# The weights of the query and key norms: a load with strides of zero, or a matmul that spreads one row

## The chip, the cores and the metric

The kernel runs on one core of a Trainium2 chip. The metric is the device time of one launch in microseconds, lower is better. The profile is one execution, taken by the hardware profiler; its engines are PE (TensorE's matmuls), PEld (TensorE's weight loads), DVE (VectorE), ACT (ScalarE), POOL (GpSimd) and SP (SyncE, which here only issues loads). SPq and ACTq are the issues of loads and stores by SP and ACT. L942 is line 942 of the kernel before.

## The reference

A backbone of two layers over 256 latent tokens and 256 context tokens of width 1024. Each layer has three token mixers on one normalised input (attention, an RWKV recurrence, a short convolution), a gated merge, and a mixture of 16 experts. All is float32. The part that the change touches is the norm of the queries and keys in the attention: each head of 64 values is divided by its root mean square and multiplied by 64 weights, which all 8 query heads share, and all 2 key heads share another 64.

```python
def _rms_norm(x, gain):
    xf = x.astype(jnp.float32)
    y = xf * lax.rsqrt(jnp.mean(xf * xf, axis=-1, keepdims=True) + NORM_EPS)
    return (y * gain.astype(jnp.float32)).astype(x.dtype)
...
        q = _rms_norm(q.reshape(b, t, ATT_HEADS, ATT_HEAD_DIM), q_gain)
        k = _rms_norm(k.reshape(b, t, ATT_KV_HEADS, ATT_HEAD_DIM), k_gain)
```

q_gain and k_gain have the shape (2, 64): one row of 64 float32 values, 256 bytes, for each layer.

## The kernel before, in words

One loop runs over the two layers. A layer computes the input projection, piece by piece: SP loads a piece of 128 columns of w_in (L337, tile w), ACT and DVE or POOL split it into a high and a low half (L102 and L103, whi and wlo), and TensorE multiplies (L106 to L108 in layer 0, L321 in layer 1). Between these pieces the RWKV recurrence runs, and the matmuls of the adaLN vectors (L188), whose weights come in two loads at a time (L185, tile adaw, three buffers). Query, key and value rows go to DRAM as they are made (L771, tensor qkd).

Behind the recurrence the attention begins, at L916. ACT issues the load of the rotary tables (L924, tile rope). Six times SP loads rows of qkd back (L932, tile qs, or ql in layer 1 where half of the rows is not needed), TensorE turns them with four (or two) transposes (L935) into a PSUM tile of the ring "sm", which has three buffers, and ACT or DVE copies that out (L938, tile qkv). Then the weights of the norms are loaded by ACT into gn, a tile of 128 partitions by 10 heads by 64 (L939 to L942). The source has a stride of zero over partitions and over heads, so that each partition gets the query weights eight times and the key weights twice:

```python
for h0, h1, nm in ((0, 8, "q_gain"), (8, 10, "k_gain")):
    gsrc = a[nm][l]
    nc.scalar.dma_start(gn[:, h0:h1], bass.AP(tensor=gsrc.tensor, offset=gsrc.offset, ap=[[0, 128], [0, h1 - h0], [1, 64]]))
```

ACT squares the rows (L952), DVE sums them (L953) and takes the reciprocal root (L955), and the rows are scaled by it (L964) and by gn (L969 on latent tokens, L979 on context tokens). The rotary embedding follows (L975 to L977), the split of queries (L981, L982) and keys (L989, L991), transposes (L986, L995; L987 and L996 copy them out), and the scores, the softmax and the products with the values (L1005 to L1026). Beside it the gates of the merge are projected with the same pieces of w_in (L761 and L762 finish and store one), SP fetches the other mixers' outputs (L912, tile ob_), the merge's weights (L1065, L1067, tile cw or cwt), and in layer 1 the first weights of the experts (L866, tile we). ACT also issues the load of the router's weights (L1055, tile wr).

The order on each engine is made when the program is built: a scheduler places the instructions of all these parts beside each other, by its own estimates. A load of ACT thus need not stand where its line stands: those of L924, L942 and, in layer 0, L1055 are placed long before the transposes of L935. On the chip each engine runs its list in order, and an instruction that waits holds up all behind it on its engine.

Of the kernel before, what the change touches and what calls it, by code (L numbers as in the profile page):

```python
# [9 lines left out]
F32 = mybir.dt.float32  # L10
# [3 lines left out]
AF = mybir.ActivationFunctionType  # L14
# [40 lines left out]
def build(tc, a, out):  # L55
    nc = tc.nc
    V, S, G, P = nc.vector, nc.scalar, nc.gpsimd, nc.tensor
    es = ExitStack()

    def pool(name, bufs=1, **kw):  # L60
        return tc.tile_pool(name=name, bufs=bufs, reuse_waits="tile", **kw)
# [5 lines left out]
    def ps(shape, tag):  # L67
        n = {"mm": 1, "mf": 2, "sm": 3, "ch": 2}[tag]
        return psp.tile(shape, F32, name="ps_" + tag, tag=tag, bufs=n)
# [5 lines left out]
    one = ck[:, C_ONE:C_ONE + 1]  # L75
# [214 lines left out]
    for l in range(2):  # L290
# [53 lines left out]
        with pool(f"n1{l}") as pl:  # L344
# [8 lines left out]
            else:  # L353
# [11 lines left out]
                for j in range(8):  # L365
                    pt = ps([128, T], ("sm", "ch", "sm", "mf")[j % 4])
                    h = pl.tile([128, T], F32, name="nh", bufs=4)
                    for s, c0 in STREAM:
                        for t in range(2):
                            P.matmul(pt[:, c0 + t * 128:c0 + t * 128 + 128], acc[:, c0 // 128 + t, j * 128:(j + 1) * 128], dg[:, c0 // 128 + t],  # L370
                                     start=True, stop=True)
# [7 lines left out]
        with er:  # L379
            pr = er.enter_context(pool(f"r{l}"))  # L380
# [535 lines left out]
        with ExitStack() as er:  # L916
            pr = er.enter_context(pool(f"a{l}"))
# [19 lines left out]
                    c = t * 128 - (512 if lat and i == 0 else 0)  # L937
                    (S.copy if (t + i) % 2 else V.tensor_copy)(raw[i][:, :, c:c + 128], pt[:, 2 * i:2 * i + 2])  # L938
            gn = pr.tile([128, 10, 64], F32, name="gn")  # L939
            for h0, h1, nm in ((0, 8, "q_gain"), (8, 10, "k_gain")):  # L940
                gsrc = a[nm][l]
                nc.scalar.dma_start(gn[:, h0:h1], bass.AP(tensor=gsrc.tensor, offset=gsrc.offset, ap=[[0, 128], [0, h1 - h0], [1, 64]]))  # L942
            qT = xp.tile([128, 8, NW], F32R, name="qT", tag="x")
            nrm = pr.tile([128, 3, 10, 64], F32, name="nrm", tag="PT")
            kT = pr.tile([128, 2, 2, T], F32R, name="kT")
# [3 lines left out]
            for tt in range(4):  # L949
                h0 = 8 if lat and tt < 2 else 0  # L950
# [5 lines left out]
            for tt in range(4):  # L956
                is_lat = tt >= 2
                hasq = is_lat or not lat
                h0 = 0 if hasq else 8
# [37 lines left out]
            for tt in range(2 if lat else 0, 4):  # L997
                nk = 4 if tt >= 2 else 2
                pov = ps([128, 512], "mm")
                for kv in range(2):  # L1000
                    PT = pr.tile([128, 4, 4, 128], F32, name="PT", bufs=PTB[l])
                    for p in range(4):
                        sc = ps([128, 512], "ch")
                        for q in range(2):
                            P.matmul(sc[:, :nk * 128], qT[:, 4 * kv + p, tt * 128 - n0:(tt + 1) * 128 - n0], kT[:, kv, q, :nk * 128],  # L1005
                                     start=(q == 0), stop=(q == 1))
# [11 lines left out]
                    for kt in range(nk):  # L1018
                        for ph in range(2):
                            P.matmul(pov[64 * ph:64 * ph + 64, 256 * kv:256 * kv + 256].rearrange("p (a q) -> p a q", a=2), rawv(kt, 640 + 64 * kv, 704 + 64 * kv),  # L1020
                                     PT[:, kt, ph::2],
                                     start=(kt == 0), stop=(kt == nk - 1), skip_group_check=True)
# [27 lines left out]
        with ExitStack() as er:  # L1050
# [54 lines left out]
            pr = esr.enter_context(pool(f"rt{l}", side="right"))  # L1105
# [12 lines left out]
            for si in range(NS):  # L1118
                for j in range(8):
# [3 lines left out]
                             start=True, stop=True, skip_group_check=True)  # L1123
# [177 lines left out]
        with ExitStack() as er:  # L1301
# [5 lines left out]
            for e in range(16):  # L1307
                ecur[0] = e
                pgu = []
                for _ in range(2):  # L1310
                    pp = ps([128, FW], "mf")
                    for j2 in range(4):
# [5 lines left out]
                        for jj in range(2):  # L1318
                            j = j2 * 2 + jj
                            for g in range(NG):  # L1320
                                P.matmul(pp[M * g:M * g + M], xe[e // 4][:, j, e % 4], w[:, jj, g * FW:(g + 1) * FW],  # L1321
                                         start=(j == 0), stop=(j == 7), skip_group_check=True)
# [10 lines left out]
                for j2 in range(4):  # L1333
                    w = wload()
                    for jj in range(2):
                        j = j2 * 2 + jj
                        fg, q = j // nq, j % nq
                        for g in range(NG):
                            P.matmul(pd[M * g:M * g + M], hT2[:, q, M * fg:M * fg + M], w[:, jj, g * FW:(g + 1) * FW],  # L1339
                                     start=(j == 0), stop=(j == 7), skip_group_check=True)  # L1340
# [88 lines left out]
```

## Time and profile before

| | us |
|---|---|
| three runs, median | 2376.88 |
| three runs, lowest and highest | 2373.63, 2391.97 |
| profiled execution, its own time | 2388.95 |
| profiled execution, span of its instructions | 2387.2 |

The two stretches that matter are the beginnings of the attention, at about 535 us in layer 0 and at about 1737 us in layer 1. A window gives, for a stretch, the busy time of each engine, the mean clock that TensorE was granted (1.00 is 2.4 GHz, 0.50 is 1.2 GHz), the mean busy share of the core's 16 DMA engines, and what they moved. In a timeline, the brackets at the end of a row hold the idle time before it and what ended it. The chain is the work that ended last, followed back from the program's end: it names at each time what the program waited for.

### The profile page before, as it was taken

How to read it: one execution, taken by the hardware profiler on the slowest of the kernel's cores; microseconds unless marked ns; L12 is line 12 of the kernel's file. 1: busy time of each engine (PE TensorE's matmuls, PEld its weight loads, DVE VectorE, ACT ScalarE, POOL GpSimd, SP SyncE). 2: the span in 40 equal slices, each digit the busy share in tenths (PEclk: the TensorE clock that was granted, in tenths of full speed). 3: DMA queues.
4: the chain of work that ended last, by engine and by line, in shares of the span. 5: the costliest groups of instructions: out<-in, count | busy, mean ns of one | idle time of the engine just before them, and what ended most of it. 6: DMA issues, size and time to landing. Idle time of an engine off the chain costs nothing.

```text
span 2387.2 us, 44154 instructions
## 1 busy us (share of the span) xinstructions
PE 2063.1 (86%) x18187; PEld 1307.5 (55%) x18187; DVE 988.9 (41%) x2525; ACT 702.3 (29%) x1481; POOL 211.3 (9%) x225
## 2 busy tenths in 40 slices
PE   6999999997999989999987999899958987676665
PEld 3766666664678943433322887777746943232222
DVE  4757475634746421211102768567456621000001
ACT  3442424223532522211102653433434421010001
POOL 1000000003223400000000100000132500000000
PEclk7999999998999999999999999789979988777866
DMA  8443333247258699999999344234365889999997
GB/s 278 121 124 94 100 100 95 84 124 223 67 181 265 200 362 363 419 420 419 420 420 367 107 120 143 63 111 144 104 183 162 280 347 417 416 416 417 417 417 304
DMA packets 343365, 585.73 MB, mean 245 GB/s; under 512 B 23550, under 2 KB 206588, under 8 KB 342908
## 3 DMA queue, kind: packets, MB, share of 16 engines
q1 hardware_dynamic: 326928, 567.69, 65.1%
q10 hardware_dynamic: 16236, 15.22, 1.9%
q8 instruction: 143, 2.34, 0.4%
q14 instruction: 58, 0.48, 0.1%
HBM read 563.44 MB, written 19.40 MB: 244 GB/s over the span
## 4 chain that ended last, share of the span: by engine, by line
PE 45%; DMA 24%; DVE 6%; ACT 2%; issue 2%; POOL 1%; SPq 1%; DVEq 0%; ACTq 0%; POOLq 0%
PE ps_mf L1321 9%; DMA we<-in_exp_down_dram 8%; DMA we<-in_exp_up_dram 6%; PE ps_mf L321 5%; DMA we<-in_exp_gate_dram 5%; PE ps_mm L1339 4%; PE ps_mf L106 3%; PE ps_mf L107 3%; PE ps_mf L108 3%; PE ps_mm L321 2%; DMA adaw<-in_ada_w_dram 2%; PE ps_ch L1163 2%; PE ps_mf L188 1%; PE ps_mm L1020 1%; PE ps_sm L534 1%
## 5 line engine op out<-in xcount | busy, mean ns | idle before, releaser
L1321 PE MATMUL ps_mf<-we,xe 128*32 128x256 f32 (+1 forms) x3040 | 414.1, 525 | 98.8 <-DMA we<-in_exp_up_dram 52.8
L1321 PEld LDWEIGHTS ps_mf<-we,xe 128*32 128x32 f32 (+1 forms) x3040 | 135.8, 133 | 341.3 <-issue 150.3
L1339 PE MATMUL ps_mm<-we,hT 128*32 128x256 f32 (+1 forms) x1536 | 201.9, 518 | 47.9 <-DMA we<-in_exp_down_dram 34.4
L102 ACT ACTIVATE whi<-w 128x512 fp32r<-128x512 f32 x236 | 147.7, 629 | 246.8 <-PE ps_mf L107 70.8
L1326 DVE TENSOR_TENSOR hid<-hid,ps_mf 128x512 f32<-128x512 f32 (+1 forms) x32 | 17.7, 554 | 443.2 <-PE ps_mf L1321 442.5
L103 DVE TENSOR_TENSOR wlo<-w,whi 128x512 fp32r<-128x512 f32 x195 | 134.0, 690 | 110.6 <-ACT whi L102 99.6
L321 PE MATMUL ps_mf<-hT,whi 128*128 128x256 f32 x736 | 157.2, 307 | 7.5 <-ACT whi L102 5.3
L1339 PEld LDWEIGHTS ps_mm<-we,hT 128*32 128x32 f32 (+1 forms) x1536 | 68.1, 133 | 164.5 <-issue 71.6
L106 PE MATMUL ps_mf<-hhi,whi 128*128 128x512 f32 x344 | 151.5, 440 | 1.3 <-ACT qs L770 0.5
L107 PE MATMUL ps_mf<-hlo,whi 128*128 128x512 f32 x344 | 142.3, 414 | 0.0
L108 PE MATMUL ps_mf<-hhi,wlo 128*128 128x512 f32 x344 | 141.3, 411 | 1.0 <-issue 1.0
L1345 DVE TENSOR_TENSOR yg<-ps_mm,g2p 128x512 f32<-128x512 f32 (+1 forms) x32 | 17.9, 558 | 275.7 <-PE ps_mm L1339 275.7
L321 PEld LDWEIGHTS ps_mf<-hT,whi 128*128 128x128 f32 x736 | 121.8, 203 | 17.3 <-ACT whi L102 5.7
L321 PE MATMUL ps_mf<-hT,wlo 128*128 128x256 f32 x368 | 109.7, 309 | 2.8 <-POOL wlo L103 1.8
L188 PE MATMUL ps_mf<-adaw,cs 128*32 128x256 f32 x640 | 82.2, 412 | 20.2 <-DMA adaw<-in_ada_w_dram 15.9
L1349 ACT COPY ye<-yg 32x512 f32<-32x512 f32 (+1 forms) x64 | 32.6, 509 | 222.9 <-DVE yg L1345 221.0
L1331 ACT ACTIVATE hT<-ps_sm 128x512 f32<-128x512 f32 (+1 forms) x32 | 15.7, 490 | 243.4 <-PE ps_sm L1330 243.4
L106 PEld LDWEIGHTS ps_mf<-hhi,whi 128*128 128x128 f32 x344 | 66.2, 193 | 24.7 <-issue 4.5
L321 PEld LDWEIGHTS ps_mf<-hT,wlo 128*128 128x128 f32 x368 | 72.5, 202 | 10.6 <-POOL wlo L103 2.6
L108 PEld LDWEIGHTS ps_mf<-hhi,wlo 128*128 128x128 f32 x344 | 66.6, 193 | 17.5 <-issue 3.8
L107 PEld LDWEIGHTS ps_mf<-hlo,whi 128*128 128x128 f32 x344 | 66.7, 194 | 14.4 <-issue 4.3
L321 PE MATMUL ps_mm<-hT,whi 128*128 128x256 f32 x368 | 70.5, 299 | 0.9 <-POOL hm L387 0.4
(472 smaller groups left out, 3789.9 us busy)
## 6 DMA issues: line engine op xcount, KB each, us to landing
we<-in_exp_down_dram SPq DMA_DIRECT2D x123, 1024.0 KB
we<-in_exp_gate_dram SPq DMA_DIRECT2D x118, 1024.0 KB
we<-in_exp_up_dram SPq DMA_DIRECT2D x117, 1024.0 KB
w<-in_w_in_dram SPq DMA_DIRECT2D x228, 256.0 KB
adaw<-in_ada_w_dram SPq DMA_DIRECT2D x160, 256.0 KB
we<-in_exp_gate_dram SPq DMA_DIRECT2D x40, 256.0 KB
adaw<-in_ada_w_dram SPq DMA_DIRECT2D x16, 512.0 KB
cw<-in_w_out_dram SPq DMA_DIRECT2D x32, 256.0 KB
```

What stands on the lines that cost most here:

```text
L102: S.activation(hi, src, AF.Copy)
L103: (eng or G).tensor_tensor(lo, src, hi.bitcast(F32), op=ALU.subtract)
L106: P.matmul(o, lh[0], rh[0], start=first, stop=False)
L107: P.matmul(o, lh[0], rh[1], start=False, stop=False)
L108: P.matmul(o, lh[1], rh[0], start=False, stop=last)
L188: P.matmul(pm[32 * g:32 * g + 32], cs[:, j, :], ws[g // 2][:, g % 2], start=True, stop=True, skip_group_check=True)
L321: P.matmul(o[:, 256 * s - c0:256 * s - c0 + 256], w_[:, j], hT[s][x][:, k], start=first and i == 0 and 256 * s == c0, stop=last and i == 2 ...
L534: P.matmul(pa[h][:, u, :nr], bkh(u4 * 4 + u, h), ARu[hh, u4 * 4 + u, :nr], start=True, stop=True)
L1163: P.matmul(pg, htok[si][:, t, j * 128:(j + 1) * 128], oh[:, t].rearrange("p e c -> p (e c)"), start=(t == 0), stop=(t == 1))
L1321: P.matmul(pp[M * g:M * g + M], xe[e // 4][:, j, e % 4], w[:, jj, g * FW:(g + 1) * FW], start=(j == 0), stop=(j == 7), skip_group_check=True)
L1339: P.matmul(pd[M * g:M * g + M], hT2[:, q, M * fg:M * fg + M], w[:, jj, g * FW:(g + 1) * FW], start=(j == 0), stop=(j == 7), skip_group_che ...
L1349: (S.copy, V.tensor_copy)[(g + si) % 2](ye[32 * eg:32 * eg + 32, si, g * FW:(g + 1) * FW], yg[p0:p0 + 32])
```

## The change

The row of 64 query weights and the row of 64 key weights are each loaded once, into one partition (tile gr). A matmul with a stationary operand of one row of ones (a column of the constants, read 128 times) and gr as the moving operand puts a copy of both rows into each partition of a PSUM tile (pgn, ring "sm"). Two ACT copies write them to gn, one reading the query row eight times, the other the key row twice. Behind it nothing is changed; from L943 on the lines of the changed file are four further down, so that L952 of before is its L956.

```diff
             gn = pr.tile([128, 10, 64], F32, name="gn")
-            for h0, h1, nm in ((0, 8, "q_gain"), (8, 10, "k_gain")):
-                gsrc = a[nm][l]
-                nc.scalar.dma_start(gn[:, h0:h1], bass.AP(tensor=gsrc.tensor, offset=gsrc.offset, ap=[[0, 128], [0, h1 - h0], [1, 64]]))
+            gr = pr.tile([1, 2, 64], F32, name="gr")
+            pgn = ps([128, 2, 64], "sm")
+            for i, (h0, h1, nm) in enumerate(((0, 8, "q_gain"), (8, 10, "k_gain"))):
+                nc.scalar.dma_start(gr[:, i], a[nm][l][None, :])
+            P.matmul(pgn.rearrange("p i x -> p (i x)"), one[0:1].to_broadcast([1, 128]), gr.rearrange("p i x -> p (i x)"), start=True, stop=True)
+            S.activation(gn[:, 0:8], pgn[:, 0:1].to_broadcast([128, 8, 64]), AF.Copy)
+            S.activation(gn[:, 8:10], pgn[:, 1:2].to_broadcast([128, 2, 64]), AF.Copy)
             qT = xp.tile([128, 8, NW], F32R, name="qT", tag="x")
```

On ACT in layer 0 this stands at the loads, before the change (thd_226 is the DRAM tensor of the gates):

```order
L924 DMA rope<-in_const_dram 128x256
L762 DMA thd_226<-th 128x512
L942 DMA gn<-in_q_gain_dram 128x8x64
L942 DMA gn<-in_k_gain_dram 128x2x64
L1055 DMA wr<-in_w_router_dram 128x8x16
L102 ACTIVATE whi<-w_6018 128x512
```

and this with the change:

```order
L924 DMA rope<-in_const_dram 128x256
L762 DMA thd_226<-th 128x512
L943 DMA gr<-in_q_gain_dram 1x64
L943 DMA gr<-in_k_gain_dram 1x64
L1059 DMA wr<-in_w_router_dram 128x8x16
L102 ACTIVATE whi<-w_6018 128x512
```

The loads keep their place; each writes one partition and not 128. In layer 1 it is the same between rope and L761, with no wr behind it.

On TensorE in layer 1, with the change, the new matmul stands behind the last group of L935 (qs is the tile of rows of qkd; hT and whi, wlo are the operands of the projection):

```order
L321 MATMUL ps_mf<-hT,whi 128x256 x2
L935 MATMUL ps_sm<-ck,qs 128x128 x4
L321 MATMUL ps_mf<-hT,wlo 128x256
L321 MATMUL ps_mf<-hT,whi 128x256 x2
L935 MATMUL ps_sm<-ck,qs 128x128 x4
L944 MATMUL ps_sm<-gr,ck 128x128
L321 MATMUL ps_mf<-hT,wlo 128x256
```

L944 is the only instruction that TensorE has more. In layer 0 it stands likewise behind the sixth group of L935, ahead of L108.

On ACT in layer 1, with the change, the two copies stand behind the last copy of L938 and ahead of the second square (here L956):

```order
L938 COPY qkv_16657<-ps_sm 128x2x128
L956 ACTIVATE nrm<-qkv_16656 128x128
L938 COPY qkv_16656<-ps_sm 128x2x128
L945 ACTIVATE gn<-ps_sm 128x512
L946 ACTIVATE gn<-ps_sm 128x128
L956 ACTIVATE nrm<-qkv_16656 128x128
L102 ACTIVATE ohC<-ob__17205 128x256
```

In layer 0 they stand ahead of the third of four squares. In both layers some instructions of the attention and of the projection beside it have changed places behind this point.

## Rows read from the trace of the kernel before

**Rows 1.** The page, busy time of each engine and its share of the span
```profile
PE 2063.1 (86%) x18187; PEld 1307.5 (55%) x18187; DVE 988.9 (41%) x2525; ACT 702.3 (29%) x1481; POOL 211.3 (9%) x225
```

**Rows 2.** Windows of layer 0: stretch, length, busy of engines, clock, DMA share, GB/s
```profile
543.30:554.30 11.00, 0.00 (x0) 0.00 (x0) 1.29 (x2) 1.63 (x3) 0.00 (x0) 0.72 0.40 117
554.30:558.30 4.00, 3.99 (x13) 2.76 (x14) 0.85 (x2) 0.65 (x2) 0.77 (x2) 0.50 0.95 305
558.30:660.00 101.70, 92.14 (x503) 63.98 (x501) 75.00 (x185) 55.33 (x134) 32.67 (x28) 0.98 0.45 144
```

**Rows 3.** Windows of layer 1, columns: PE, PEld, DVE, ACT, POOL, clock, DMA, GB/s
```profile
1740.30:1755.40 15.10, 0.00 (x0) 0.00 (x0) 0.28 (x1) 0.00 (x0) 0.00 (x0) 0.58 0.29 85
1755.40:1759.60 4.20, 4.17 (x20) 4.17 (x21) 0.85 (x2) 1.38 (x3) 1.28 (x1) 0.50 0.82 239
1759.60:1843.00 83.40, 64.84 (x407) 51.26 (x407) 60.96 (x125) 41.52 (x98) 27.68 (x26) 0.89 0.65 198
```

**Rows 4.** Timeline of PE at both places: start us, us, instruction, idle before
```profile
542.64 0.62 PE L188 MATMUL ps_mf<-adaw,cs 128*32 128x256 f32 x4
554.31 1.07 PE L188 MATMUL ps_mf<-adaw,cs 128*32 128x256 f32 x4 [11.05 <-DMA adaw<-in_ada_w_dram]
...
1740.00 0.28 PE L321 MATMUL ps_mf<-hT,wlo 128*128 128x256 f32 x1
1755.43 0.69 PE L935 MATMUL ps_sm<-ck,ql 128*128 128x128 f32 x2 [15.16 <-DMA ql<-qkd]
```

**Rows 5.** Timeline of SP's issues, layer 0, then layer 1
```profile
536.13 5.86 SPq L185 DMA_DIRECT2D adaw<-in_ada_w_dram  x2
...
1739.16 15.16 SPq L932 DMA_DIRECT2D ql<-qkd  x4
```

**Rows 6.** DMA queues, 1739.5 to 1749, then 538.5 to 549: packets, MB, share
```profile
q10 hardware_dynamic: 698, 0.18, 7.0%
q1 hardware_dynamic: 63, 0.03, 1.2%
...
q10 hardware_dynamic: 734, 0.19, 6.6%
q1 hardware_dynamic: 29, 0.06, 2.0%
```

**Rows 7.** Timeline of ACT's issues, layer 0, then layer 1
```profile
534.83 0.45 ACTq L942 DMA_DIRECT2D gn<-in_q_gain_dram  x1
537.32 0.39 ACTq L942 DMA_DIRECT2D gn<-in_k_gain_dram  x1
537.74 7.06 ACTq L1055 DMA_DIRECT2D wr<-in_w_router_dram  x1
...
1737.11 0.46 ACTq L942 DMA_DIRECT2D gn<-in_q_gain_dram  x1
1737.99 0.39 ACTq L942 DMA_DIRECT2D gn<-in_k_gain_dram  x1
```

**Rows 8.** Pieces of the chain that ended last: start us, us, what
```profile
509.25 2.87 DMA adaw<-in_ada_w_dram
...
572.24 4.66 DMA ob__7113<-oRd
...
577.56 0.64 ACT nrm L952
...
1758.16 4.83 DMA ob__17274<-oCd
...
1763.34 0.73 ACT nrm L952
```

**Rows 9.** Lines L935, L987 and L989: shortest, median, longest ns of one
```profile
L935 PE MATMUL ps_sm<-ck,qs x32: 270/273/477, 555.3 to 1761.4; 128*128 128x128 f32 x32
...
L987 ACT ACTIVATE qT<-ps_sm x12: 591/596/606, 592.2 to 1796.5; 128x512 fp32r<-128x512 f32 x12
L989 ACT ACTIVATE ks<-nrm x16: 292/294/310, 589.7 to 1793.4; 128x128 fp32r<-128x128 f32 x16
```

## The prediction

> **What bounds the kernel now.** I read the share of each engine first: TensorE is busy for 86% of the span [rows 1], so what a small change is worth depends on where TensorE stands still. I then read windows of a few microseconds around the two loads that the change replaces, one pair in each layer. In layer 0 TensorE does nothing at all between 543.3 and 554.3 us, and in layer 1 nothing between 1740.3 and 1755.4 us [rows 2, 3]. In the second stretch no engine does more than one small operation, and the DMA engines are busy for 0.29 of it only. So nothing is the bound there: everything waits for something that moves no data.
>
> The timeline says for what. In layer 0 the matmul of L188 sits idle for 11.05 us until its adaw load has landed; in layer 1 the transpose of L935 sits idle for 15.16 us until the first ql has landed [rows 4]. Both loads are ordinary ones of SP, and SP had asked for them in time: at 536.13 and 538.00 (two issues merged in one row, 5.86 us long) and from 1739.16 on [rows 5]. The four ql issues of layer 1 took 15.16 us together, so SP itself was held up while it issued. What ran meanwhile is in the DMA views of the two stretches [rows 6]: 698 packets on q10 with 0.18 MB, which is 256 bytes a packet, against 63 packets on q1; in layer 0, 734 against 29. A row of 64 float32 is 256 bytes, so these packets are the gain loads of L942, which ACT issued at 534.83 and 537.32, and at 1737.11 and 1737.99 [rows 7]. They were 1,280 packets a layer (128 partitions times 10 heads), they went through at 698 in 9.5 us, about 73 per us, and together they kept 7% of 16 engines busy, about one engine of the sixteen. At that rate 1,280 take 17.5 us, which covers both stalls. While they pass, SP's loads hardly move. I take that as the cause; how the two queues come to hold each other up, these rows do not tell.
>
> **The change part by part.** It removes the 1,280 packets of each layer and puts two loads of 64 numbers in their place, issued by ACT at the same two places of its order. The sum for one layer after the other, against the profiled execution's own time, 2388.95 us:
>
> Layer 0. The waiting L188 needs the second adaw of the pair that was asked for at 538.00. How long such a load takes when nothing is in its way is bounded by two pieces of the chain: 2.87 us at 509.25, and 4.83 us for a load in a full queue at 1758.16 [rows 8]. It then lands between 540.9 and 542.8, before TensorE gets to it at 543.26, so all of the 11.05 us goes. What is late next is TensorE itself. It also came out of the stall at half its clock: 0.50 was granted for 554.3 to 558.3, with 3.99 us of TensorE work in it [rows 2]; in 558.3 to 660 the grant was 0.98. That level came after the idle stretch, and without it the same work takes 2.0 us less. Layer 0: 11.05 + 2.0 = 13.05 us. Its other end is 11.05, if the clock falls anyway.
>
> Layer 1. The first ql is asked for at 1739.16 and lands at 1742.03 with the shorter latency, 1743.99 with the longer. TensorE is out of work at 1740.28, so 1.75 (or 3.71) us of waiting stays and 15.16 - 1.75 = 13.4 us goes (or 11.45). I take 13.4, because two loads of weights at most stand ahead of ql on SP's queue. The half clock (0.50 from 1755.4 to 1759.6, with 4.17 us of work) is worth less here: the chain soon leaves TensorE for a load that SP issues at 1758.16 [rows 8], so only the 2.7 us from 1755.43 on count, and I put 1.0 us on it, between 0 and 2.1. Layer 1: 14.4 us.
>
> Added, per layer: one 128 x 128 matmul (L944 of the changed file) behind the last group of L935; the same shape at L935 is 0.27 us with 0.14 us of weight load beside it [rows 9], so 0.3 us on TensorE, nought if it falls into a gap. Two ACT copies out of PSUM: a 128 x 512 one takes 0.60 us at L987 and a 128 x 128 one 0.29 us at L989 [rows 9], so 0.9 us. They read one row of 64 repeated eight times (and twice), which no row of before shows on ACT; I bound them by 0.9 us and twice that. They stand on ACT ahead of the squares of L952, and the chain runs through L952 in both layers, at 577.56 and at 1763.34 [rows 8]; so I count them in full. Both layers: 2 x (0.3 + 0.9) = 2.4 us, between 0 and 4.2.
>
> What else waits: L944 is in TensorE's order and waits for gr; behind it stand the L108 or L321 matmuls and, over them, everything. The two gr loads take the place of issues at 534.83 and 537.32, and the first group of L935 comes at 555.3, or 544.3 with the stall out of between, with five more groups and much of the projection behind it until L944 [rows 7, 9]; a load takes 2.87 to 4.83 us, so the wait is nought. In layer 1 the lead runs from 1737.99 to 1742.03 and over all groups of L935, which take from 1755.43 to 1761.4 [rows 4, 9], so about 10 us, still enough. pgn takes a third of the "sm" buffers until the two copies are done; the next users of that ring are the transposes of L986, which stand behind the whole norm. The load wr of layer 0 (L1055), which was held for 7.06 us while ACT issued it, goes out at once. The scheduler places work of the attention stages a little differently (some 40 places on ACT and 60 on TensorE); I cost that at nothing on the mean and allow 3 us either way.
>
> Sum: 13.05 + 14.4 - 2.4 = 25.05 us. All that follows hangs on these two points, since no engine and no load made headway in the stalls that could be late instead. So 2388.95 - 25 = 2363.9 us for the profiled execution. That one lies 12.1 us above the median of the three runs, 2376.88, which range from 2373.63 to 2391.97; the stall has no reason to differ between them, so I take the 25 us from the median: 2351.8, that is 2352 us, or 1.05% less. About 1%, some 24 us, is what a measurement of this kernel can tell from no change, and the forecast is hardly beyond that.
>
> **Rivals.** The stall is not the gain loads' doing. The packets kept one engine's worth of sixteen busy, and nothing shows that this alone must hold SP's loads; then the time stays at 2376.88 plus the 2.4 us of added work at most, 2377 to 2379. Against it: the same loads stand at the same place in both layers, and in layer 1 no wr load stands behind them. The Trainium skill, in "DMA: Bandwidth & Descriptors", section "Issuing engines are not separate DMA queues", says that loads issued from SP and ACT run on the same sixteen engines and interleave. By that rule q1's packets would take turns with the gain packets, and the stall would be another's. The trace does not agree: 63 packets of q1 beside 698 [rows 6].
>
> Part is given back. The stage behind each stall is the attention, which runs on waits between DVE, ACT and TensorE and on loads. If the longer latency holds in layer 1 (11.45), the clock falls anyway (no 3.0) and the added work is 4.2, the gain is 11.05 + 11.45 - 4.2 = 18.3 us and the time 2358.6; if one of the two stalls stays in another shape, it is about 13 - 1.2, so 2365.
>
> More comes back: layer 0 has pieces of 4.66 us at 572.24 and, in layer 1, of 4.83 us at 1758.16 [rows 8], loads behind the backlog that the stall left. If they fall to 2.87 us, the gain is 25 + 1.8 + 2.0 = 29 us, 2348; with no added cost on the chain, 2345.6.
>
> Slower: the other order of the attention stage. TensorE is idle there for 101.70 - 92.14 = 9.6 us in layer 0 and 83.40 - 64.84 = 18.6 us in layer 1 [rows 2, 3], 28 us. A copy or a transpose that is queued one step later lengthens each of these waits. If the idle time doubles, that costs 28 us against 25 and the time is 2380; it decides from 25 us more on. Against it: the moved instructions are few, and none but L944 to L946 is new.
>
> **How the numbers follow.** The forecast (both stalls go, 20 to 28 us) has 0.62, more than that 0.10, part given back 0.20, no effect 0.05, slower 0.03. The line of 1% lies at 23.8 us, inside the forecast: I put 0.47 of its 0.62 beyond it and, with the 0.10, 0.57 on faster by over 1%; the slower rival at 2380 is itself within 1%, of its 0.03 half reaches beyond, which I round to 0.02; the rest, 0.41, is within 1%. The range goes down to 2340 (the largest gain, 2345.6, less the 3 us by which a run lay under the median, and 2 of reordering) and up to 2370 (one stall left, 2365, and 5 us of scatter), so it leaves out no effect, slower and the tails, some 0.15.
>
> **What would show it.** In the changed profile: no idle stretch of TensorE over 4 us at the adaw and ql loads; SP issues there of 0.3 to 0.4 us each; no 256-byte packets in hundreds on q10; wr issued in under 1 us in layer 0; a granted clock of 1.00 through both places; two new ACT copies of 0.6 and 0.3 us. I am wrong if an idle stretch of over 8 us stands at either place still, or if it is gone and the span is less than 15 us shorter.

## The result, and the profile after

The changed kernel took 2354.11 us (median of four runs, 2348.76 to 2359.97), beside 2383.33 us for the kernel before on the same chip (four runs, 2373.63 to 2391.97): a ratio of 0.9883, with a 95% interval of 0.9851 to 0.9916. The profiled execution took 2359.37 us, its span is 2357.6 us, against 2388.95 and 2387.2 before: 29.6 us less.

TensorE is busy for 7.7 us less than before [rows 1], which is 0.4% of its work; the other 21.9 us are time in which it stood still. Line of the page with the share of the engines, changed kernel:

```profile
PE 2055.4 (87%) x18191; PEld 1299.7 (55%) x18191; DVE 993.1 (42%) x2525; ACT 703.5 (30%) x1485; POOL 208.8 (9%) x225
```

Timeline of PE, changed kernel: the place of the wait in layer 0, the longest wait for adaw behind it, then the first ql of layer 1.

```profile
541.28 0.64 PE L188 MATMUL ps_mf<-adaw,cs 128*32 128x256 f32 x8
...
553.47 0.62 PE L188 MATMUL ps_mf<-adaw,cs 128*32 128x256 f32 x4 [1.71 <-DMA adaw<-in_ada_w_dram]
...
1727.45 0.69 PE L935 MATMUL ps_sm<-ck,ql 128*128 128x128 f32 x2 [1.98 <-DMA ql<-qkd]
```

The waits of 11.05 and 15.16 us of [rows 4] are gone. In layer 0 the matmuls that stood on either side of the wait, at 542.64 and 554.31 us, now run as one row of eight without a break; the 1.71 us stand at a later L188, which waited 1.16 us before. In layer 1, 1.98 us stand where 15.16 were. SP's timeline, same two issues as in [rows 5]:

```profile
534.47 2.48 SPq L185 DMA_DIRECT2D adaw<-in_ada_w_dram  x2
...
1724.12 2.43 SPq L932 DMA_DIRECT2D ql<-qkd  x4
```

The two issues of adaw took 0.33 us each, with a wait for a semaphore between them. Four issues of ql took 2.43 us together instead of 15.16, 0.32 to 0.90 us each. ACT's issues, to be read beside [rows 7]: the two small loads, and wr behind them, which was held for 7.06 us before.

```profile
533.17 0.30 ACTq L943 DMA_DIRECT2D gr<-in_q_gain_dram  x1
533.51 0.28 ACTq L943 DMA_DIRECT2D gr<-in_k_gain_dram  x1
535.93 0.40 ACTq L1059 DMA_DIRECT2D wr<-in_w_router_dram  x1
```

DMA queues of 1723 to 1728 in the changed kernel: packets, MB, share of 16 engines.

```profile
q1 hardware_dynamic: 1587, 1.02, 69.6%
q10 hardware_dynamic: 110, 0.09, 5.4%
```

In 5 us SP's queue (q1) moved 1,587 packets; before it was 63 in 9.5 us [rows 6]. The new instructions, by line, shortest, median and longest ns of one:

```profile
L944 PE MATMUL ps_sm<-gr,ck x4: 270/320/371, 559.6 to 1733.7; 1*128 1x128 f32 x4
...
L945 ACT ACTIVATE gn<-ps_sm x2: 598/599/600, 560.2 to 1734.0; 128x512 f32<-128x512 f32 x2
...
L946 ACT ACTIVATE gn<-ps_sm x2: 272/274/277, 560.7 to 1734.5; 128x128 f32<-128x128 f32 x2
```

L944 shows as two instructions a layer and not as one, 0.48 us together. A copy that reads one PSUM row of 64 eight times takes what a plain copy out of PSUM of that size takes, 0.60 us [rows 9]; the smaller one took 0.27 us. Whether they cost time is told by the chain that ended last, changed kernel, where they stand (start us, us, what; layer 0, then layer 1, ahead of which stands the first ql):

```profile
557.90 5.49 DMA ob__7118<-oRd
...
563.42 0.03 ACT ohR L102
...
563.96 0.73 ACT nrm L956
...
1724.12 3.29 DMA ql<-qkd
...
1732.84 5.54 DMA w<-in_w_in_dram
...
1738.47 0.64 ACT whi L102
```

L944 to L946 run between 559.6 and 561.0 us, and between 1733.7 and 1734.8. In both places the chain is inside a load, so they lie beside it.

Where in the program the 29.6 us came from is read off lines that stand around the two places. In layer 0 these are the last matmul of L147, at about the time of the load's issue, and the last product with the values (L1020 of before, L1024 of the changed kernel); in layer 1 they are the last L188 and the end of the program. Before, then changed:

```profile
L147 PE MATMUL ps_mf<-ck,adas x2: 273/286/299, 535.1 to 535.3; 128*128 128x128 f32 x2
...
L1020 PE MATMUL ps_mm<-PT,qkv x96: 378/379/431, 615.8 to 674.7; 128*64 128x256 f32 x96
...
L188 PE MATMUL ps_mf<-adaw,cs x640: 378/403/637, 91.7 to 1697.7; 128*32 128x256 f32 x160
```

```profile
L147 PE MATMUL ps_mf<-ck,adas x2: 273/286/299, 533.5 to 533.6; 128*128 128x128 f32 x2
...
L1024 PE MATMUL ps_mm<-PT,qkv x96: 379/379/431, 604.7 to 662.2; 128*64 128x256 f32 x96
...
L188 PE MATMUL ps_mf<-adaw,cs x640: 379/403/637, 90.9 to 1682.7; 128*32 128x256 f32 x160
```

The stretch of layer 0 took 139.4 us and now takes 128.6, 10.8 less. That of layer 1 took 689.5 us and now takes 674.9, 14.6 less. The remaining 4.2 us lie ahead of and between the two stretches, in code that did not change.

Inside layer 0 more was won at the place itself, and part of it was given back. Windows from one L188 ahead of the place to the next L188 behind the first L935, with the same 80 matmuls in both, before and then changed (stretch, length, PE, PEld, DVE, ACT, POOL, granted clock, DMA share, GB/s):

```profile
533.41:562.80 29.39, 17.14 (x80) 11.29 (x79) 4.52 (x10) 4.91 (x10) 3.36 (x4) 0.83 0.58 179
...
531.75:548.00 16.25, 14.78 (x80) 10.00 (x79) 4.44 (x10) 5.04 (x10) 3.37 (x4) 1.00 0.94 289
```

The place gave 13.1 us: 11.05 us of waiting, and 2.4 us by which the same matmuls are shorter at full clock, less some small waits. Behind it stands a wait that the kernel before does not have:

```profile
575.04 0.79 PE L106 MATMUL ps_mf<-hhi,whi 128*128 128x512 f32 x1 [3.43 <-DVE adas L192]
```

DVE's L192, which reads the PSUM tile of the adaLN matmuls and for which TensorE waits there, comes 7.2 us after its matmuls (567.38 to 574.57 us); before it came 3.3 us after them (580.90 to 584.15 us). In DVE's new order two more instructions of the norm stand ahead of it, and the chain that ended last runs through them. TensorE's clock fell as well; windows of the changed kernel, to be read beside [rows 2, 3]:

```profile
541.90:560.00 18.10, 16.39 (x93) 11.73 (x89) 6.97 (x14) 8.59 (x18) 5.14 (x4) 1.00 0.92 292
560.00:575.00 15.00, 8.43 (x46) 5.12 (x45) 11.90 (x22) 7.69 (x16) 8.78 (x7) 0.84 0.81 253
575.00:600.00 25.00, 21.58 (x108) 15.39 (x109) 20.91 (x36) 12.25 (x29) 11.80 (x12) 0.89 0.45 139
600.00:647.00 47.00, 46.74 (x260) 31.88 (x259) 36.75 (x118) 27.49 (x76) 5.41 (x5) 1.00 0.17 51
...
1720.00:1727.40 7.40, 5.13 (x41) 4.72 (x39) 0.77 (x2) 2.44 (x5) 2.63 (x3) 1.00 0.68 201
1727.40:1729.40 2.00, 1.95 (x9) 1.96 (x10) 0.16 (x1) 1.00 (x2) 1.22 (x1) 0.50 0.87 269
1729.40:1731.40 2.00, 2.00 (x14) 2.00 (x13) 0.69 (x2) 0.60 (x2) 0.05 (x1) 0.66 0.87 261
1731.40:1733.40 2.00, 2.00 (x18) 1.83 (x17) 0.42 (x1) 0.92 (x3) 1.29 (x1) 1.00 0.82 247
```

Layer 0 comes through its place at full clock, but then TensorE works only 8.43 of 15 us and the grant falls there: 0.84 for 15 us and 0.89 for 25. Between the levels of 0.50 and 1.00 that is 2 x (0.16 x 15 + 0.11 x 25) = 10.3 us at half clock; in the 105.7 us of before it was 2 x (0.50 x 4.0 + 0.02 x 101.7) = 8.1 us. In layer 1 half clock still follows the short wait, for 2.0 + 1.4 us.

### The profile page after: what moved, and what is told of

It reads as the page before. It is cut to its first block, busy times and chain, and to the rows that moved or that the text cites. A ratio compares the mean times of both kernels' runs of the same rounds, so it can differ in the third digit from the quotient of the medians.

```text
span 2357.6 us, 44171 instructions
## 1 busy us (share of the span) xinstructions
PE 2055.4 (87%) x18191; PEld 1299.7 (55%) x18191; DVE 993.1 (42%) x2525; ACT 703.5 (30%) x1485; POOL 208.8 (9%) x225
## 4 chain that ended last, share of the span: by engine, by line
PE 46%; DMA 23%; DVE 6%; ACT 2%; issue 1%; POOL 1%; SPq 1%; DVEq 0%; ACTq 0%; POOLq 0%
PE ps_mf L1325 9%; DMA we<-in_exp_down_dram 9%; DMA we<-in_exp_up_dram 7%; PE ps_mf L321 5%; DMA we<-in_exp_gate_dram 5%; PE ps_mm L1343 4%; PE ps_mf L106 3%; PE ps_mf L107 3%; PE ps_mf L108 3%; PE ps_mm L321 2%; PE ps_ch L1167 2%; PE ps_mf L188 1%; PE ps_mm L1024 1%; PE ps_sm L534 1%; PE ps_sm L1020 1%
## 5 line engine op out<-in xcount | busy, mean ns | idle before, releaser
L106 PE MATMUL ps_mf<-hhi,whi 128*128 128x512 f32 x344 | 151.4, 440 | 5.3 <-DVE adas L192 4.6
L108 PE MATMUL ps_mf<-hhi,wlo 128*128 128x512 f32 x344 | 140.9, 410 | 1.5 <-issue 1.5
L188 PE MATMUL ps_mf<-adaw,cs 128*32 128x256 f32 x640 | 80.3, 410 | 9.4 <-DMA adaw<-in_ada_w_dram 5.2
L106 PEld LDWEIGHTS ps_mf<-hhi,whi 128*128 128x128 f32 x344 | 66.2, 192 | 30.8 <-issue 6.1
L108 PEld LDWEIGHTS ps_mf<-hhi,wlo 128*128 128x128 f32 x344 | 66.3, 193 | 17.0 <-issue 3.0
L103 POOL TENSOR_TENSOR wlo<-w,whi 128x512 fp32r<-128x512 f32 x41 | 54.8, 1337 | 188.4 <-ACT whi L102 115.5
```

What stands on the lines that cost most here:

```text
L103: (eng or G).tensor_tensor(lo, src, hi.bitcast(F32), op=ALU.subtract)
L106: P.matmul(o, lh[0], rh[0], start=first, stop=False)
L108: P.matmul(o, lh[1], rh[0], start=False, stop=last)
L188: P.matmul(pm[32 * g:32 * g + 32], cs[:, j, :], ws[g // 2][:, g % 2], start=True, stop=True, skip_group_check=True)
```

## The experiments

The theory after this reading: the load of before asks 1,024 times for the query row and 256 times for the key row, reads of one row pass at a fixed slow rate, and while they pass SP's loads do not. Its rivals: it is the number of small packets; it is the stride of zero as such; it is the other order of the instructions. The first four kernels keep the whole change and add a load into a tile that nobody reads, so that little but the reads differs. Each of them ran once, and beside them the kernel before, 2382.66 us. Runs of one kernel scatter by some 10 us to either side, so these four are judged by their waits and not by their times.

**The old load put back.** In all four the tile is `gd`, and the two issues stand just ahead of gr's:

```diff
+            gd = pr.tile([128, 10, 64], F32, name="gd")
...
+                nc.scalar.dma_start(gd[:, h0:h1], bass.AP(tensor=gsrc.tensor, offset=gsrc.offset, ap=[[0, 128], [0, h1 - h0], [1, 64]]))
```

> The changed kernel, and beside it the old load with strides of zero into a tile that nothing reads, issued by ACT at the same place in both layers. If the 1,280 packets themselves hold the queues up, both stalls are back: TensorE idle over 9 us at the adaw load of layer 0 and over 11 us at the ql load of layer 1, about 73 packets per us on q10, and the span 20 to 30 us over that of the changed kernel (2357.6). If the stall came from the order of the instructions or from waiting for gn, nothing reads the new tile, and the span stays within 8 us of 2357.6 with no idle stretch over 4 us.

Measured: 2376.27 us. Timeline of PE, then the DMA queues of 1730 to 1740:

```profile
549.34 1.07 PE L188 MATMUL ps_mf<-adaw,cs 128*32 128x256 f32 x4 [10.06 <-DMA adaw<-in_ada_w_dram]
...
1744.29 1.97 PE L935 MATMUL ps_sm<-ck,ql 128*128 128x128 f32 x8 [14.56 <-DMA ql<-qkd]
```

```profile
q10 hardware_dynamic: 835, 0.21, 7.9%
q1 hardware_dynamic: 137, 0.07, 2.4%
```

Both stalls are back though gn no longer depends on the load: nobody waits for the load itself, they come from what it does to SP's loads. 835 packets in 10 us are 84 per us. The span, 2374.5 us, is only 16.9 us over the change's and not 20 to 30; but the two stretches named above took 143.5 and 687.6 us, 27.6 us more than with the change, and the rest of this execution was shorter.

**As many packets, each from an address of its own.** gw is w_in of the layer, W_ the length of one of its rows.

```diff
+                nc.scalar.dma_start(gd[:, h0:h1], bass.AP(tensor=gw.tensor, offset=gw.offset, ap=[[8 * W_, 128], [W_, h1 - h0], [1, 64]]))
```

> The changed kernel, and beside it 1,280 packets of 256 bytes into a tile that nothing reads, each from an address of its own (rows of w_in). If the number of small packets is what holds the queues up, the stalls are back as with the old load, at about 73 packets per us, 20 to 30 us. If it is reading one address again and again, they pass many times faster (wr, 1,024 packets of 64 bytes, goes through at some 500 per us), the stall is under 4 us in each layer and the span within 10 us of 2357.6.

Measured: 2359.63 us. DMA queues of 1720 to 1722, then PE:

```profile
q10 hardware_dynamic: 1201, 0.30, 66.6%
q1 hardware_dynamic: 474, 0.24, 41.7%
```

```profile
550.69 0.63 PE L188 MATMUL ps_mf<-adaw,cs 128*32 128x256 f32 x4 [3.69 <-DMA adaw<-in_ada_w_dram]
...
1723.82 1.97 PE L935 MATMUL ps_sm<-ck,ql 128*128 128x128 f32 x8 [3.14 <-DMA ql<-qkd]
```

The same 1,280 packets of 256 bytes pass at 600 per us, and SP's queue moves 474 beside them. Number and size of the packets alone are out.

**A stride of zero over the heads alone.**

```diff
+                nc.scalar.dma_start(gd[:, h0:h1], bass.AP(tensor=gw.tensor, offset=gw.offset, ap=[[8 * W_, 128], [0, h1 - h0], [1, 64]]))
```

> The changed kernel, and beside it 1,280 packets of 256 bytes, of which each partition reads one row of its own eight times, then twice: the stride of zero over heads alone. If the repeated address costs by how often one address is read in all (128 x 10 before, 8 here), the packets pass fast and the span stays within 10 us of 2357.6. If repeats directly behind one another are what is slow, or the number of packets, the stalls are back, 20 to 30 us.

Measured: 2352.64 us; DMA queue of 1713 to 1715:

```profile
q10 hardware_dynamic: 1136, 0.28, 62.7%
```

568 per us, and 3.42 us of waiting for ql at most. A zero stride with 128 different addresses, each read ten times, brings no stall.

**A stride of zero over partitions, with one long row.** Each partition reads the same row of 640 numbers, in two pieces; gw is ada_b here.

```diff
+                nc.scalar.dma_start(gd[:, h0:h1], bass.AP(tensor=gw.tensor, offset=gw.offset + 64 * h0, ap=[[0, 128], [64, h1 - h0], [1, 64]]))
```

> The changed kernel, and beside it one row of 640 consecutive numbers read by all 128 partitions: the stride of zero over partitions alone, few and long packets (128 of 2 KB, 128 of 512 bytes). If one address read 128 times is slow by itself at 13.7 ns a read (73 per us), 128 reads are 1.8 us and the two loads 3.5 us, of which TensorE sees under 3 us a layer: span within 10 us of 2357.6. If any stride of zero over partitions blocks the queues for long, the stalls are back at over 8 us.

Measured: 2363.21 us. PE waits 3.79 us for adaw and 2.79 us for ql, so neither stall is there. DMA queue of 1723 to 1724:

```profile
q10 hardware_dynamic: 103, 0.18, 50.1%
```

Reads of one place go at about 100 per us here too, though most of them carry 2 KB and not 256 bytes; the 256 reads are over in some 3 us. That the price is one per read and not per byte is not shown by this run: with SP's queue the sixteen engines are busy for 0.85 of that microsecond, so the bytes can be the limit as well. Reads of 256 bytes at about this rate come with the kernel that reads each row once per partition, below.

**The change in layer 0 alone, and in layer 1 alone.** The other layer keeps the old load.

```diff
+            if l == 0:
+                gr = pr.tile([1, 2, 64], F32, name="gr")
...
+            else:
+                for h0, h1, nm in ((0, 8, "q_gain"), (8, 10, "k_gain")):
```

> The change in layer 0 alone. If each stall is worth what the prediction's terms say, layer 0 gives 13.05 - 1.2 = 11.9 us: a ratio to before of 0.995 (0.9935 to 0.997), the stall of layer 1 still there at 13 to 16 us. If what comes free in layer 0 is given back in the attention behind it, as the two traces hint (TensorE 11.9 us earlier at the first L935, but 8 us at the experts), it is 0.9965 or nearer to 1. If the order of the instructions is what helps, nothing can be said by layers.

> The change in layer 1 alone. By the prediction's terms 14.4 - 1.2 = 13.2 us, a ratio of 0.9945 (0.993 to 0.996), the stall of layer 0 still there at 10 to 13 us. The two ratios' gains should add up to that of the whole change (1.17%); if one of them is near nothing, its stall hid other work.

Measured, with the kernel before at 2378.05 us (14 runs): layer 0 alone 2367.43 us (7 runs), ratio 0.9942 (0.9918 to 0.9965); layer 1 alone 2368.86 us (8 runs), ratio 0.9940 (0.9914 to 0.9965). Each keeps the stall of the other place, as a row of PE of each shows:

```profile
1733.26 0.69 PE L935 MATMUL ps_sm<-ck,ql 128*128 128x128 f32 x2 [14.12 <-DMA ql<-qkd]
```

```profile
553.08 1.07 PE L188 MATMUL ps_mf<-adaw,cs 128*32 128x256 f32 x4 [10.17 <-DMA adaw<-in_ada_w_dram]
```

0.58% and 0.60% are 13.8 and 14.3 us of 2378; together 1.18%, and the whole change had 1.17%. So near a match is luck: each interval is 5 to 6 us to either side, and the medians alone lie 10.6 and 9.2 us apart. What the runs show is that each place is worth something by itself, and the stretches below that each has its own stall.

**Each row read once per partition, without the matmul.** The kernel before, with 256 packets a layer instead of 1,280, and two copies from SBUF.

```diff
-            for h0, h1, nm in ((0, 8, "q_gain"), (8, 10, "k_gain")):
+            gr = pr.tile([128, 2, 64], F32, name="gr")
+            for i, (h0, h1, nm) in enumerate(((0, 8, "q_gain"), (8, 10, "k_gain"))):
                 gsrc = a[nm][l]
-                nc.scalar.dma_start(gn[:, h0:h1], bass.AP(tensor=gsrc.tensor, offset=gsrc.offset, ap=[[0, 128], [0, h1 - h0], [1, 64]]))
+                nc.scalar.dma_start(gr[:, i], bass.AP(tensor=gsrc.tensor, offset=gsrc.offset, ap=[[0, 128], [1, 64]]))
+                S.activation(gn[:, h0:h1], gr[:, i:i + 1].to_broadcast([128, h1 - h0, 64]), AF.Copy)
```

> The kernel before with a third way to the same values: each row is read once by each partition (stride of zero over partitions alone, 128 packets of 256 bytes a row), and two ACT copies repeat it over the heads. No matmul, no PSUM tile. If reads of one address pass at about 75 per us, 256 of them take 3.4 us and hold SP's loads so long: TensorE idle 1 to 4 us at both places and a time within 5 us of the changed kernel (ratio 0.986 to 0.992). If the stall is due to a stride of zero over partitions as such, it is back and the ratio is over 0.997.

Measured: 2356.51 us (6 runs), ratio 0.9895 (0.9865 to 0.9924); 3.43 us of waiting for ql, no long stall. Not told apart from the change: the gain needs fewer reads of one address, not the matmul. DMA queues of 1714 to 1715, while these reads pass:

```profile
q1 hardware_dynamic: 478, 0.24, 85.4%
q10 hardware_dynamic: 96, 0.02, 10.0%
```

The reads of 256 bytes pass at 96 per us (107 in the microsecond before), much as in the other loads of one address, but here SP's queue moves 478 packets beside them. So the low rate is there with 128 reads of each row as well, and it does not stop SP's loads by itself.

**No load of weights at all.** The kernel before without the loads; POOL sets gn to 8.0, so the weights of the norms are left out.

```diff
-            for h0, h1, nm in ((0, 8, "q_gain"), (8, 10, "k_gain")):
-                gsrc = a[nm][l]
-                nc.scalar.dma_start(gn[:, h0:h1], bass.AP(tensor=gsrc.tensor, offset=gsrc.offset, ap=[[0, 128], [0, h1 - h0], [1, 64]]))
+            G.memset(gn, 8.0)
```

> The kernel before without any load of the two rows: POOL fills gn with 8.0, so the weights of the norms are left out. It has neither the stall nor the matmul and copies, and so bounds what can be won here. If the added work of the change costs the 2.4 us of the prediction, it is 2 to 3 us faster than the changed kernel (ratio 0.986 to 0.989); if it costs nothing, both are the same; if the rearranged order of the attention has cost some of the gain, this kernel is over 5 us faster than the changed one.

Measured: 2354.25 us (6 runs), ratio 0.9884 (0.9851 to 0.9917). With matmul, copies and loads gone the time is the change's own. The interval is some 8 us to either side, so a cost of 2 us could not be seen in it; that there is none is the reading of the chain above. Nor does this kernel tell what the new order in layer 0 costs, though that was expected of it: TensorE's wait for L192 stands in it too, with 2.19 us.

**Ten addresses, each read by all partitions.** The changed kernel and a load as in the second experiment, with another stride:

```diff
+                nc.scalar.dma_start(gd[:, h0:h1], bass.AP(tensor=gw.tensor, offset=gw.offset + W_ * h0, ap=[[0, 128], [W_, h1 - h0], [1, 64]]))
```

> The changed kernel with one load per layer added into a tile that nobody reads: again 1,280 packets of 256 bytes with a stride of zero over the 128 partitions, but each of the ten heads reads another row of the experts' weights, so that ten addresses are read 128 times each instead of one 1,280 times. Theory one (reads of one address pass one after the other at about 75 packets per us; reads of other addresses pass beside them): the packets pass several times faster than 75 per us, at 300 to 700, TensorE has no idle piece over 4 us at the adaw loads or the ql loads, span within 10 us of 2357.6. Rival (any load with a stride of zero over partitions and short rows passes slowly): about 75 packets per us, both stalls of 10 to 15 us back, span 2375 to 2385.

Measured: 2366.38 us, span 2364.6. DMA queue of 1727 to 1729, then PE:

```profile
q10 hardware_dynamic: 1082, 0.27, 60.4%
```

```profile
558.01 0.63 PE L188 MATMUL ps_mf<-adaw,cs 128*32 128x256 f32 x4 [4.22 <-DMA adaw<-in_ada_w_dram]
...
1731.05 2.29 PE L935 MATMUL ps_sm<-ck,ql 128*128 128x128 f32 x8 [3.34 <-DMA ql<-qkd]
```

The rows are those of w_in, not of the experts' weights as the expectation has it. 541 per us with ten addresses against 84 with one: several times the rate, as the theory wanted. The wait of 4.22 us, at the L188 that waits 1.71 us with the change, is just over its bound of 4, and the span is inside its 10 us.

**The old load later, behind the norm.** It takes gn's place once gn is used (same tag, one buffer), so that it is issued during the attention.

```diff
-            gn = pr.tile([128, 10, 64], F32, name="gn")
+            gn = pr.tile([128, 10, 64], F32, name="gn", tag="gn")
...
+            gd = pr.tile([128, 10, 64], F32, name="gd", tag="gn")
...
+                nc.scalar.dma_start(gd[:, h0:h1], bass.AP(tensor=gsrc.tensor, offset=gsrc.offset, ap=[[0, 128], [0, h1 - h0], [1, 64]]))
```

> The changed kernel with the old load of the gains (1,280 packets that read one address, stride of zero) added into a tile that takes the place of the gain tile once the norm has used it, so that it is issued after the norm, during the attention, and nobody waits for it. Theory one (the load costs only what SP has to bring in the same 17 us or so): the packets pass again at about 75 per us, SP's loads of that stretch are held up as before, but fewer of them are wanted at once: TensorE's idle time at the adaw loads and ql loads of the old places stays under 4 us, and the time lies between the change and before, 2358 to 2375. Rival (the load costs the same wherever it stands): two stalls of 10 to 15 us at other loads, span 2375 to 2385.

Measured: 2356.91 us (one run), span 2355.1: just under the expected range. DMA queues of 585 to 595, all of them; SP; then the longest waits of PE beside the load in layer 0 and in layer 1; and L188:

```profile
q10 hardware_dynamic: 788, 0.20, 7.4%
```

```profile
590.87 14.84 SPq L337 DMA_DIRECT2D w<-in_w_in_dram  x4
```

```profile
588.97 1.06 PE L990 MATMUL ps_sm<-ck,qs 128*128 128x128 f32 x8 [1.24 <-DVE qs L986]
...
1759.19 0.80 PE L321 MATMUL ps_mf<-hT,whi 128*128 128x256 f32 x2 [8.54 <-ACT whi L102]
...
L188 PE MATMUL ps_mf<-adaw,cs x640: 379/403/637, 90.3 to 1664.7; 128*32 128x256 f32 x160
```

Here nothing else moved for 10 us, and the load still went at 79 per us: the low rate does not come from sharing with SP's loads. SP was held as before (four issues in 14.84 us), but in layer 0 TensorE had enough in SBUF: the stretch of layer 0 took 128.0 us, as with the change. In layer 1 it was otherwise. TensorE waited for whi three times, 8.54 us at the longest and 11.8 us in all, where the change has one such wait of 3.45 us; and from the last L188, at 1664.7 us, to the end it took 690.4 us, 15.5 us more than with the change and as much as with the load at its old place; kernels without the old load took 674.9 to 683.5 us there. The whole time hides this: at 1664.7 us this execution was 18.0 us ahead of the change's, 17.4 of them in code that is the same in both. So the load issued later, at 583.8 instead of about 525 us and at 1741.2 instead of about 1704, cost nothing in layer 0 and did cost in layer 1; the rival is out for the one and not for the other.

**The change once more.**

> The changed kernel once more, unchanged, beside the kernel before: every theory expects the ratio of 0.985 to 0.992 again, with runs that scatter by some 10 us between 2349 and 2360.

Measured: 2355.72 us (7 runs, 2347.25 to 2364.66) beside 2375.15 (10 runs, 2363.27 to 2386.85), ratio 0.9912 (0.9878 to 0.9946). With the first measurement, the gain is 0.9% to 1.2%.

**The two stretches in each trace.** Single executions, in us; in layer 1, from the last L188 to the first transpose of ql, and from the same L188 to the end.

| kernel | layer 0 | layer 1, to ql | layer 1, to the end |
|---|---|---|---|
| before | 139.4 | 57.7 | 689.5 |
| old load put back | 143.5 | 57.4 | 687.6 |
| change in layer 1 alone | 141.3 | 45.0 | 675.5 |
| change in layer 0 alone | 126.3 | 56.8 | 689.1 |
| the change | 128.6 | 44.7 | 674.9 |
| the change once more | 126.5 | 44.7 | 676.7 |
| each row once per partition | 126.4 | 46.2 | 683.5 |
| no load of weights | 127.7 | 45.8 | 680.5 |
| old load later | 128.0 | 44.8 | 690.4 |

These scatter less than the whole time. Without the old load at its place layer 0 is shorter by 11 to 17 us, and layer 1 by 11 to 13 us up to ql.

## Why the prediction was right, and where it was not

Forecast: 2352 us, 1.05% less. Measured 2354.11 us, 1.17% less in one comparison and 0.88% in the other; between the medians that is 29.2 and 19.4 us, against 25 forecast. That it lies beyond the 1% is as open as it was put. That the time itself agrees to 2 us is in part luck, as the kernel before took 2383.33 us in that comparison and not the 2376.88 from which the forecast was taken.

**The cause.** Shown: with the load back both stalls are back, with its reads spread over other addresses they are not. The rival by which the stall was another's is out (it wanted 2377 to 2379). It named a rule: the Trainium skill, in "DMA: Bandwidth & Descriptors", section "Issuing engines are not separate DMA queues", says that loads from different engines run on the same sixteen DMA engines and interleave. The traces agree with that rule for reads of different addresses, where SP's queue moved 474 packets beside 1,201, and for 128 reads of each of two addresses, 478 beside 96. They do not agree for the old load, with 1,024 reads of one address and 256 of another: 137 beside 835.

**The stalls.** Layer 0: all of the 11.05 us goes, and no wait is left between those matmuls. Layer 1: 1.75 us was to stay; 1.98 us is there, and the first ql took 3.29 us on the chain, nearer to the 2.87 us that were taken than to 4.83. Both steps held.

**The half clock.** Layer 0: "without it the same work takes 2.0 us less" came true at the place, where the same 80 matmuls are busy for 2.4 us less and 13.1 us were won, with 13.05 forecast. It did not last: the low grant came back some 20 us later and takes 10.3 us instead of 8.1. Layer 1: 1.0 us was counted; it is 3.4 us at half clock against 4.2 in [rows 3], so about half of 0.8, 0.4 us. "A granted clock of 1.00 through both places" came true in layer 0 only.

**The order of the attention.** "I cost that at nothing on the mean": this step failed. DVE's L192 stands further back in the new order of layer 0, and TensorE waits for it, 3.43 us in the changed kernel, with half clock behind it. In all eleven traces in which layer 0 is changed such a wait is there, 2.19 to 3.64 us; in the two in which it is not, before and the change in layer 1 alone, L106 has no wait of even 0.9 us there. It is there with the old load put back too, 3.19 us, so it belongs to the order and not to the missing stall. Of the 13.1 us 10.8 are left at the end of layer 0's attention.

**The added work.** "The chain runs through L952 in both layers, so I count them in full", 2.4 us. The two copies took the 0.9 us that were forecast, though the row of L989 that stood for the smaller one reads SBUF and not PSUM; L944 took 0.48 us instead of 0.3. The place was not right: the chain reaches L956 (L952 of before) from a load of 5.49 us in layer 0, and in layer 1 a load of 5.54 us covers them. That earlier work stands ahead of an instruction on its engine does not put it on the chain.

**The sum.** The terms that were off have opposite signs: 2.4 us of work were not paid, and of what was won at layer 0's place 2.3 us were given back, with 0.6 us of clock in layer 1. By stretches the gain is 10.8 and 14.6 us in the two profiled executions, against 13.05 - 1.2 and 14.4 - 1.2 forecast. That the two together, 25.4, come so near to 25.05 is luck, as these stretches differ by up to 9 us between kernels without the old load.

**The other rivals.** Part given back: some 2 us in layer 0's attention, through its new order, but not a stall in another shape. More comes back: the loads behind the backlog were to fall from 4.66 and 4.83 to 2.87 us; the loads on the chain there take 5.49 and 5.54 us, with the sixteen engines 0.92 and 0.87 busy. Slower through the other order: the wait for L192 is of this kind, but it is 3.43 us and not the 25 that were needed.

Left open: why SP's loads stand while the old load passes. The runs show that they do and how long, not in which part of the chip. The old load differs from the others in two things, the 1,024 reads of one address and the two zero strides in one pattern; every other load has at most 128 reads of one address and at most one zero stride, so the runs do not tell these two apart. It is not that one DMA engine does all the work: 7.4% of sixteen is 1.2 engines, and the load of ten addresses, with the same zero stride over the partitions, kept 60.4% busy. Nor is it the place of the rows in memory, from which the kernel that reads each row once per partition loads without a stall.

## What to carry to other kernels

A load with zero strides can cost far more than its bytes: count how often the busiest address is read. Here 1,024 reads of one row and 256 of another stopped SP's loads for some 10 us, and 128 reads of each did not; between these no run was made. Where the count is high, read the row once and spread it on the chip, or let each partition read it once and repeat it with a copy. A transfer that shows as 7% of the DMA engines' time can stand beside a queue that has stopped, so look at the packets beside a stall by queue, not at the DMA share. To issue such a load later is no sure cure: in single traces it cost nothing in layer 0 and some 7 to 16 us in layer 1. And where the runs of one kernel scatter by as much as the change is worth, compare stretches of the traces around the place, not one whole time.

## What the runs showed that was not expected

Reads of one address pass slowly: 70 and 73 per us in the kernel before, 84 with the old load put back, 79 with no other packet moving, which is one in 12 to 14 ns, and 96 to 107 where two rows are read 128 times each. Ten addresses pass at 541, 128 at 568 and 1,280 at 600 per us. While the old load passes SP's queue moves fewer and fewer packets: with the old load put back, whose packets start at 1728.4 us, 78, 57, 15 and 4 in the microseconds from 1729 on, and none in the six behind them. And TensorE's grant fell to 0.50 behind a wait of only 1.98 us, in the first 2 us after it; in the 7.4 us before, the wait among them, at 1.00, TensorE had worked for 5.13.
